# Starting addresses of the slots that TensorE reads, moved to multiples of 256 bytes

## The chip, the cores and the metric

One core of a Trainium2 chip runs the whole program. The metric is device time in microseconds (us) from the start to the end of one execution. The kernel before was run three times; the profile is one further execution of it.

## The reference

Two blocks of two layers each are applied to 512 tokens of width 1024, all in float32. What matters here is where the products are:

```python
# first block, layer l (x: [512, 1024])
h = rms_norm(x, norm_mix[l]);  z = h @ w_in[l]          # 1024 x 2560
# grouped attention, a gated recurrence in both directions and a gated convolution on parts of z
x = x + concatenate([o_att, o_hg, o_cv]) @ w_out[l]     # 1024 x 1024
h = rms_norm(x, norm_mlp[l])
x = x + square(relu(h @ w_mlp_in[l])) @ w_mlp_out[l]    # 1024 x 4096, 4096 x 1024
# second block, layer l: four mixers (sparse attention, stick breaking, gated linear, forgetting attention),
# each through a branch product 512 x 1024 times a gate; w_out_2, then the same kind of feed forward
```

## The kernel before, in words

The residual stream is kept transposed: features on the 128 partitions, 512 tokens along the free dimension, in 8 tiles. TensorE multiplies in the type float32r, which takes the leading bits of a float32 word, so each operand is split in a leading and a trailing part (`split`, L304: a copy on ScalarE and a subtraction on VectorE), and each product is made of three: leading by leading, leading by trailing, trailing by leading (`mm3`, L338).

Weights come by DMA in pieces of [128, 512] words (`wload`, L314) to slots `wr`, and are split to `wh` and `wl`. One unit holds four weight tiles of 128 x 128. `product` (L344) then takes 12 products of 512 columns with each unit: the weight tile is loaded into the array (the profile's PEld), and a part of the source is streamed past it. The source is the normed input (`xh`, `xl`: `tlater`, L366), the hidden layer of the feed forward (`hid`: `mlp`, L492), or the mixed heads (`mxh`, `mxl`: `out_proj`, L519, and the branches, L1984). `nlater` (L370) takes narrow products the other way round: a tile of `xh` or `xl` is loaded, and 256 columns of weights are streamed past it.

The feed forward of a layer runs alone: four times, 8 tiles of 128 hidden features are made from the input (8 x 8 x 3 = 192 products), and then 8 tiles of the output from these (192 products). The mixers run with projections in between, which are queued and emitted in small steps by a pacing rule (`Core.step`, L258). The order on each engine is fixed when the program is built.

Where a slot stands in SBUF follows from the pools. `Core.__init__` (L163) opens the pool `core` with the identity, the residual tiles, `xh`, `xl` and small vectors, and `corew` with the weights. `Core.scope` (L189) opens for each block a pool of small things and one of slots of [128, 512] words by purpose (`SLOTS_1`, L112, and `SLOTS_2`, L113), from which `Core.t` (L212) takes tiles; slots of the purpose k are 32 words wider. Each pool starts where the one before it ends, and a tile's size is rounded up to 32 bytes. So one small vector moves everything that stands behind it.

Of the kernel before, what the change touches and what calls it, by code (L numbers as in the profile page):

```python
# [29 lines left out]
T = 512          # tokens  # L30
D = 1024         # model width
# [5 lines left out]
AHEAD = 1        # units of weights that are loaded ahead  # L37
PARTS = 2        # steps in which the products with a unit of weights are emitted

# ---------------------------------------------------------------- constants of the shapes  # L40


def _const_parts():
    p = np.arange(128)[:, None]
    f = np.arange(128)[None, :]
    tok = np.arange(T).reshape(NT, 128).T          # [128, NT]
    parts = {}
    parts["ident"] = (p == f)
    parts["causal"] = np.where(f > p, NEG, 0.0)                       # query p, key f
    parts["far"] = np.where(f <= p, NEG, 0.0)                         # key tile two before the query's  # L50
# [3 lines left out]
    parts["sbm"] = (p < f)                                            # key p, query f  # L54
    parts["sbb"] = np.where(p >= f, NEG, 0.0)
    parts["tri"] = np.where(p >= f, -1.0, 0.0)                        # key' p, key f
# [9 lines left out]
    # axial rope of the first block: cos and signed sin for each token and feature  # L66
# [38 lines left out]
# ---------------------------------------------------------------- the program  # L105

# PSUM banks by purpose; each block has one more
BANKS = dict(pm=2, ps=2, pt=2, po=1)
# buffers of weights: as loaded, leading parts, trailing parts
WEIGHTS = dict(wr=4, wh=4, wl=3)  # L110
# slots of [128, T] words by purpose, of the first and of the second block
# [4 lines left out]
class Later:  # L116
    """work for the tensor engine that is emitted in small steps between those of something else. units: pairs of
    functions, of which the first loads weights, and the second (a generator) takes the products with them;
    finish: what to do at the end"""
# [7 lines left out]
    def load(self, n=1):  # L127
        """the weights of the next n units; how many are left to others"""
        while n and len(self.ws) < len(self.units):
            self.ws.append(self.units[len(self.ws)][0]())  # L130
            n -= 1
        return n

    def advance(self, alone=False):
        """the next step; alone: no weights are loaded for what follows"""
# [26 lines left out]
class Core:  # L162
    def __init__(self, ctx, tc, const):  # L163
# [10 lines left out]
        self.ident = self.cload("ident", self.cp)  # L174
        self.x = [self.xtile() for k in range(KT)]
# [10 lines left out]
        self.keep = tc.dram_tile([KT, 128, T], F32, name="keep")  # L186

    # -- memory
    def scope(self, ctx, name, bank, **bufs):  # L189
        """the memory of one block: slots of [128, T] by purpose, one more bank for a purpose"""  # L190
        pool = lambda n, **k: ctx.enter_context(self.tc.tile_pool(name=name + n, bufs=1, **k))
        self.ps = {bank: pool("p", space=PSUM)}
        self.bp, self.gp = pool("c"), pool("g")
        self.sp = self.bp
        self.bufs, self.turn = bufs, {}

    def next(self, name, n, times=1):
        """0, 1, .. n - 1 by turns, each some times in a row"""
# [13 lines left out]
    def t(self, tag, name="t", dt=F32, shape=None):  # L212
        """a slot of [128, T] words (k: 32 more)"""
        w = T + 32 if tag == "k" else T
# [19 lines left out]
    def vec(self, v, name, kt):  # L234
        """a vector of kt*128 features, features on the partitions"""
# [10 lines left out]
    # -- work in between  # L246
# [21 lines left out]
    def ahead(self, work, u):  # L268
        """load the weights for the unit after u of some work"""
# [13 lines left out]
    def rsqrt(self, out, ms, n):  # L283
        """1/sqrt of a small positive tile: through the logarithm, then a step of Newton's"""
# [9 lines left out]
    def norm_rows(self, weights, squares, r):  # L294
        """r = 1/sqrt of the squares' sums by weights over the partitions, plus EPS, in every row"""
# [7 lines left out]
    # -- products in float32r parts  # L303
    def split(self, hi, lo, src, hi_in=None):  # L304
        """src = hi + lo exactly, hi with the leading 12 bits"""
# [8 lines left out]
    def wload(self, pieces, a, b):  # L314
        """pieces: [(DRAM AP, their rows, their columns)]; the weights' a tiles [128, b], each in two parts"""
# [17 lines left out]
    def wcols(self, w, k0=0, kt=KT):  # L333
        """rows k0*128.. of w, [.., its columns]"""
# [9 lines left out]
    def product(self, w, n, src, finish, extra=None):  # L344
        """finish(w.T @ src) for 128 columns of n * 128 rows of weights; src: k -> the parts of its rows [128, tokens];
        extra: what else to load"""
# [19 lines left out]
    def tlater(self, w, finish=lambda p: p):  # L366
        """(x g) @ w for 128 columns, transposed: [columns, tokens]"""
        return self.product(w, KT, lambda k: (self.xh[k], self.xl[k]), finish)

    def nlater(self, w, finish=lambda ps: ps):  # L370
        """(x g) @ w for 256 columns, [tokens, columns]: two banks of two token tiles each.
        w: AP [1024, 256]; finish: of the [128, 256] products of the token tiles"""
# [27 lines left out]
    # -- residual stream, kept transposed  # L400
    def load_x(self, x, g, tag):
        """x [tokens, features] to features on the partitions; the tokens' squares are summed on the way"""
# [31 lines left out]
    def parts_of(self, k, g, x):  # L434
        """x times the norm's weight, in two parts; the row scale follows the products"""
# [9 lines left out]
    def prep(self, k, g, spill=False):  # L445
        """x[k] is final"""
# [5 lines left out]
    def rows(self, col, n=128):  # L452
        """a column [128 tokens, NT] as rows: out[p, t] = col[t], in PSUM"""
# [5 lines left out]
    # the row scale of the norm, along the tokens in every row and as columns; taken from the squares at its first use  # L459
# [1643 lines left out]
```

## Time and profile before

| | us |
|---|---|
| the three runs | 3782.01, 3783.26, 3784.59; median 3783.26 |
| the profiled execution: span from the first to the last instruction | 3781.8 |
| TensorE busy in it | 3664.3 (97%) |
| VectorE, ScalarE, GpSimd busy | 2319.6 (61%), 1900.7 (50%), 948.4 (25%) |

The median of the runs is 1.5 us above the profiled span. A row of the profile names an engine (PE is TensorE's product, PEld its weight load, DVE VectorE, ACT ScalarE, POOL GpSimd), the line of the kernel, the operation, and its tiles as output<-inputs. Of a product's two inputs, a row gives the streamed one first in the groups `pm<-xh,wh` and `pm<-hid,wh`, and in `pm<-wh,xh` of the narrow products too. The shape behind the names, 128x512, is what is streamed. Products overlap: the next one starts while the one before is still on its way, so a product's time in a row is longer than the distance between two starts.

### The profile page before, as it was taken

Reading aid. Unit: us, or ns where it says so; the run is one execution under the profiler, and the core shown is the slowest. Engines: PE = TensorE matmul, PEld = TensorE weight load, DVE = VectorE, ACT = ScalarE, POOL = GpSimd, SP = SyncE. Lnnn points to the kernel's source line nnn. Section 1 sums busy time; section 2 is a strip of 40 time slices with the busy share of each in tenths; the row PEclk is TensorE's granted clock in tenths of the full one; section 3 lists DMA queues with packets and bytes.
Section 4 is the critical chain, followed back from the end, with each engine's and each line's share of the span. In section 5 each row is a group of like instructions: output and inputs, shape, how many; then the busy total and the mean of one; then the engine's idle time right before and its main releaser. Section 6 shows DMA issues by size and latency. Waiting matters only on the chain.

```text
span 3781.8 us, 53178 instructions
## 1 busy us (share of the span) xinstructions
PE 3664.3 (97%) x18793; PEld 3006.3 (79%) x18793; DVE 2319.6 (61%) x4554; ACT 1900.7 (50%) x3940; POOL 948.4 (25%) x925
## 2 busy tenths in 40 slices
PE   8889999988999999999999999999999999999999
PEld 7757888885688887888788888887888888888887
DVE  7885333599543346787778763335588777874334
ACT  6575333466643333677654643334567844553333
POOL 4732222466122230001213122222001121222222
PEclk9999999998999999999999999999999999999999
DMA  4102333321133344212222233334312222233332
GB/s 127 53 12 79 92 95 95 114 57 31 43 93 94 93 114 129 54 46 73 67 71 68 71 112 96 96 95 123 100 34 68 71 67 71 64 104 94 96 95 87
DMA packets 561851, 306.65 MB, mean 81 GB/s; under 512 B 49978, under 2 KB 551344, under 8 KB 561584
## 3 DMA queue, kind: packets, MB, share of 16 engines
q1 hardware_dynamic: 558128, 296.95, 28.6%
q10 hardware_dynamic: 3456, 6.29, 0.5%
q8 instruction: 148, 2.42, 0.3%
q14 instruction: 119, 0.97, 0.1%
HBM read 292.68 MB, written 10.49 MB: 80 GB/s over the span
## 4 chain that ended last, share of the span: by engine, by line
PE 83%; DVE 11%; ACT 2%; DMA 1%; issue 1%; SPq 0%; POOL 0%; POOLq 0%; DVEq 0%; ACTq 0%
PE pm L340 21%; PE pm L341 21%; PE pm L342 21%; PE po L637 2%; PE pm L387 2%; PE pm L386 2%; PE pm L388 2%; DVE cy L1199 2%; PE pt L619 1%; PE pa L1014 1%; DVE X L1106 1%; DVE X L1107 1%; DVE acc L1128 1%; PE pt L1951 1%; DVE nm L584 1%
## 5 line engine op out<-in xcount | busy, mean ns | idle before, releaser
L308 DVE TENSOR_TENSOR wl<-wr,wh 128x512 fp32r<-128x512 f32 x956 | 679.8, 711 | 784.9 <-issue 377.3
L307 ACT ACTIVATE wh<-wr 128x512 fp32r<-128x512 f32 x956 | 600.3, 629 | 1084.1 <-PE pm L341 949.3
L340 PE MATMUL pm<-xh,wh 128*128 128x512 f32 x2160 | 863.7, 400 | 7.9 <-DVE zq L1040 3.9
L342 PE MATMUL pm<-xh,wl 128*128 128x512 f32 x2160 | 860.7, 399 | 8.2 <-POOL wl L327 8.2
L341 PE MATMUL pm<-xl,wh 128*128 128x512 f32 x2160 | 858.9, 398 | 0.0
L342 PEld LDWEIGHTS pm<-xh,wl 128*128 128x128 f32 x2160 | 407.2, 189 | 105.2 <-POOL wl L327 11.6
L340 PEld LDWEIGHTS pm<-xh,wh 128*128 128x128 f32 x2160 | 407.4, 189 | 102.2 <-DVE zq L1040 4.4
L341 PEld LDWEIGHTS pm<-xl,wh 128*128 128x128 f32 x2160 | 407.4, 189 | 93.5 <-issue 2.8
L341 PE MATMUL pm<-hid,wh 128*128 128x512 f32 x1024 | 402.0, 393 | 0.0
L342 PE MATMUL pm<-hid,wl 128*128 128x512 f32 x1024 | 401.2, 392 | 0.0
L340 PE MATMUL pm<-hid,wh 128*128 128x512 f32 x1024 | 400.3, 393 | 0.0
L515 POOL TENSOR_TENSOR x<-x,os 128x512 f32<-128x512 f32 x124 | 207.2, 1671 | 431.0 <-DVE os L513 430.2
L504 POOL TENSOR_TENSOR s<-r 128x512 f32<-128x512 f32 x128 | 134.0, 1047 | 593.5 <-ACT r L503 551.8
L386 PE MATMUL pm<-wh,xh 128*128 128x256 f32 x896 | 257.2, 290 | 4.7 <-ACT wh L307 3.3
L387 PE MATMUL pm<-wl,xh 128*128 128x256 f32 x896 | 257.6, 289 | 2.5 <-DVE wl L308 2.2
L388 PE MATMUL pm<-wh,xl 128*128 128x256 f32 x896 | 255.7, 287 | 0.0
L342 PEld LDWEIGHTS pm<-hid,wl 128*128 128x128 f32 x1024 | 192.4, 188 | 43.8
L340 PEld LDWEIGHTS pm<-hid,wh 128*128 128x128 f32 x1024 | 192.3, 188 | 43.5
L341 PEld LDWEIGHTS pm<-hid,wh 128*128 128x128 f32 x1024 | 192.3, 188 | 43.0
L340 PE MATMUL pm<-mxh,wh 128*128 128x512 f32 x512 | 203.2, 400 | 7.7 <-ACT mxh L307 4.9
L513 DVE TENSOR_TENSOR os<-pm,R 128x512 f32<-128x512 f32 x128 | 88.5, 692 | 196.7 <-PE pm L342 196.7
L341 PE MATMUL pm<-mxl,wh 128*128 128x512 f32 x512 | 203.6, 398 | 0.6 <-DVE mxl L308 0.6
(619 smaller groups left out, 6743.8 us busy)
## 6 DMA issues: line engine op xcount, KB each, us to landing
wr<-in_w_in_dram SPq DMA_DIRECT2D x376, 256.0 KB
wr<-in_w_ff_dram SPq DMA_DIRECT2D x256, 256.0 KB
wr<-in_w_mlp_in_dram SPq DMA_DIRECT2D x128, 256.0 KB
wr<-in_w_mlp_out_dram SPq DMA_DIRECT2D x128, 256.0 KB
wr<-in_w_out_dram SPq DMA_DIRECT2D x64, 256.0 KB
wr<-in_w_branch_dram SPq DMA_DIRECT2D x64, 256.0 KB
xo<-keep SPq DMA_DIRECT2D x32, 256.0 KB
keep<-x ACTq DMA_DIRECT2D x24, 256.0 KB
```

The source lines that it names most:

```text
L307: nc.scalar.activation(hi, src, AF.Copy)
L308: nc.vector.tensor_tensor(lo, src, (hi if hi_in is None else hi_in).bitcast(F32), op=ALU.subtract)
L340: nc.tensor.matmul(out, wh, xh, start=start, stop=False)
L341: nc.tensor.matmul(out, wh, xl, start=False, stop=False)
L342: nc.tensor.matmul(out, wl, xh, start=False, stop=stop)
L386: nc.tensor.matmul(o, self.xh[kk][:, c], h, start=f, stop=False, skip_group_check=True)
L387: nc.tensor.matmul(o, self.xh[kk][:, c], l, start=False, stop=False, skip_group_check=True)
L388: nc.tensor.matmul(o, self.xl[kk][:, c], h, start=False, stop=e, skip_group_check=True)
L504: nc.gpsimd.tensor_tensor(s, r, r, op=ALU.mult)
L513: nc.vector.tensor_tensor(s, po, R2, op=ALU.mult)
L515: (nc.vector if last and m == KT - 1 else nc.gpsimd).tensor_tensor(self.x[m], self.x[m], s, op=ALU.add)
L637: nc.tensor.matmul(*x, start=start and n == 0, stop=stop and n == len(mm) - 1, skip_group_check=True)
```

## The change

Four paddings and two wider slots. A padding of 128 bytes stands behind the identity in the pool `core`, one of 96 bytes is the first tile of the weights' pool `corew`, and one of 160 bytes in the first block's pool of small things (0, so none, in the second's). The k slots grow from 544 to 576 words, and the convolution's padded input from 542 to 576 words, of which 542 are used as before. On every engine the instructions are the same as before, in the same order; only addresses differ. (The diff also takes comments out, which is left out here; lines from L175 on stand 1 to 10 further down.)

```diff
@@ Core.__init__
         self.ident = self.cload("ident", self.cp)
+        self.pad(self.cp, 128)
         self.x = [self.xtile() for k in range(KT)]
...
         self.keep = tc.dram_tile([KT, 128, T], F32, name="keep")
+        self.pad(self.core_w, 96)
+
+    def pad(self, pool, n):
+        pool.tile([128, n // 4], F32, name="pad", tag=f"pad{n}", bufs=1)
@@ Core.scope
-    def scope(self, ctx, name, bank, **bufs):
+    def scope(self, ctx, name, bank, before, **bufs):
...
+        if before:
+            self.pad(self.bp, before)
@@ Core.t
-        w = T + 32 if tag == "k" else T
+        w = T + 64 if tag == "k" else T
@@ First.memory, Second.memory
-        K.scope(ctx, "first", "pa", **SLOTS_1)
+        K.scope(ctx, "first", "pa", 160, **SLOTS_1)
-        K.scope(ctx, "second", "ps", **SLOTS_2)
+        K.scope(ctx, "second", "ps", 0, **SLOTS_2)
@@ First.conv
-            u = K.gp.tile([128, T + 30], F32, name="u", tag="cu", bufs=1)
+            u = K.gp.tile([128, T + 64], F32, name="u", tag="cu", bufs=1)[:, :T + 30]
```

What this does to the places in the built program. Each number is the byte within a partition at which a tile starts, modulo 256; steps within a slot from one tile to the next are 512 or 1024 bytes and change nothing in it.

| what TensorE reads | before | after |
|---|---|---|
| weights `wh`, `wl` | 32 | 0 |
| normed input `xh`, `xl` | 128 | 0 |
| hidden layer, first block | 128; trailing parts of tiles 0 to 3 at 0 | 0 |
| hidden layer, second block | 32 | 0 |
| mixed heads `mxh`, `mxl`, first block | 128 | 0 |
| mixed heads, second block | 32 | 0 |
| values and weights of the attentions and of gated linear attention, second block | 32 (a few 160 and 224) | 0 (a few 192) |
| identity | 128 | 128 |
| triangle of ones (`tri`), stick breaking | 64 | 32 |

By number of float32r products of 512 columns: before, 2784 have streamed operand and weights at the same place modulo 256 (32 and 32), 8144 have 128 and 32, and 256 have 0 and 32. After it, 11,344 have 0 and 0. Of the narrow ones of 256 columns, 2688 have 32 and 128 before, 680 have 32 and 32; after it 3472 have 0 and 0.

## Rows read from the trace of the kernel before

**Rows 1.** Page: TensorE's busy time, and its granted clock in 40 slices.
```profile
PE 3664.3 (97%) x18793; PEld 3006.3 (79%) x18793; DVE 2319.6 (61%) x4554; ACT 1900.7 (50%) x3940; POOL 948.4 (25%) x925
PEclk9999999998999999999999999999999999999999
```
**Rows 2.** Busy by stage, one layer of each block (stretch, length, PE PEld DVE ACT POOL, clock, DMA, GB/s).
```profile
0.00:330.00 330.00, 284.12 (x1580) 224.04 (x1581) 260.29 (x459) 212.84 (x438) 156.40 (x172) 0.97 0.22 63
330.00:717.20 387.20, 387.20 (x1666) 311.54 (x1665) 154.45 (x233) 138.27 (x235) 102.71 (x75) 1.00 0.35 101
...
1416.00:2234.30 818.30, 803.31 (x4597) 677.02 (x4596) 621.24 (x1456) 481.09 (x1100) 122.34 (x156) 0.99 0.29 76
2234.30:2589.50 355.20, 355.20 (x1551) 289.62 (x1551) 136.29 (x208) 123.89 (x211) 94.46 (x74) 1.00 0.36 102
```
**Rows 3.** Page: the chain of work that ended last, by engine.
```profile
PE 83%; DVE 11%; ACT 2%; DMA 1%; issue 1%; SPq 0%; POOL 0%; POOLq 0%; DVEq 0%; ACTq 0%
```
**Rows 4.** Page: groups of TensorE (xcount | busy us, mean ns | idle before).
```profile
L340 PE MATMUL pm<-xh,wh 128*128 128x512 f32 x2160 | 863.7, 400 | 7.9 <-DVE zq L1040 3.9
...
L340 PE MATMUL pm<-hid,wh 128*128 128x512 f32 x1024 | 400.3, 393 | 0.0
...
L386 PE MATMUL pm<-wh,xh 128*128 128x256 f32 x896 | 257.2, 290 | 4.7 <-ACT wh L307 3.3
...
L340 PE MATMUL pm<-mxh,wh 128*128 128x512 f32 x512 | 203.2, 400 | 7.7 <-ACT mxh L307 4.9
```
**Rows 5.** Timeline of TensorE: first products of five pieces (start us, us).
```profile
448.27 0.39 PE L340 MATMUL pm<-xh,wh 128*128 128x512 f32 x1
...
493.07 0.39 PE L340 MATMUL pm<-hid,wh 128*128 128x512 f32 x1
...
537.92 0.39 PE L340 MATMUL pm<-xh,wh 128*128 128x512 f32 x1
...
2324.52 0.40 PE L340 MATMUL pm<-xh,wh 128*128 128x512 f32 x1
...
2369.34 0.40 PE L340 MATMUL pm<-hid,wh 128*128 128x512 f32 x1
...
2412.90 0.40 PE L340 MATMUL pm<-xh,wh 128*128 128x512 f32 x1
```
**Rows 6.** Busy time in the two pieces on the hidden layer (columns as in rows 2).
```profile
493.07:537.90 44.83, 44.83 (x193) 36.10 (x192) 15.87 (x24) 11.12 (x19) 12.77 (x8) 1.00 0.32 94
...
2369.34:2412.90 43.56, 43.56 (x194) 36.03 (x192) 15.87 (x24) 11.14 (x19) 12.76 (x8) 1.00 0.33 96
```
**Rows 7.** Timeline of TensorE: eleven narrow products (L1937), then 25 of `nlater`.
```profile
1888.64 0.28 PE L1937 MATMUL po<-fl,gv 128*128 128x256 f32 x1
...
1889.95 0.40 PE L340 MATMUL pm<-mxh,wh 128*128 128x512 f32 x1
...
1894.28 0.28 PE L386 MATMUL pm<-wh,xh 128*128 128x256 f32 x1
...
1897.22 0.27 PE L1951 MATMUL pt<-X,Z 128*128 128x128 f32 x1
```
**Rows 8.** Timeline and line L1014: eight float32 products, 256 columns, not float32r.
```profile
298.11 1.89 PE L1014 MATMUL pa<-pt,va 128*64 128x256 f32 x8
L1014 PE MATMUL pa<-pt,va x7: 379/379/379, 298.1 to 299.4; 128*64 128x256 f32 x7
```
**Rows 9.** Timeline of TensorE: thirteenth and 25th product of the piece at 493.07.
```profile
495.87 0.40 PE L340 MATMUL pm<-hid,wh 128*128 128x512 f32 x1
...
498.67 0.40 PE L340 MATMUL pm<-hid,wh 128*128 128x512 f32 x1
```
**Rows 10.** Groups of weight loads: weights loaded (L340), input tiles loaded (L386).
```profile
L340 PEld LDWEIGHTS pm<-xh,wh 128*128 128x128 f32 x2160 | 407.4, 189 | 102.2 <-DVE zq L1040 4.4 <-DVE z L552 3.3 <-DVE gv L1869 2.0
...
L386 PEld LDWEIGHTS pm<-wh,xh 128*128 128x128 f32 x896 | 170.6, 192 | 9.3 <-ACT wh L307 4.4 <-issue 1.5 <-DVE z L552 1.3
```

## The prediction

> **What bounds the kernel now.** I read the page's busy shares and 40 slices first. TensorE is busy for 97% of the span, and its granted clock is 0.9 or more in 39 of the 40 slices and above 0.8 in the other [rows 1], so neither idle time nor the clock is what a change of addresses could give back. Cut at the stages, the stage windows (one layer of each block stands in the rows; the other layer of a block is like it) show feed-forward stretches in which TensorE is busy without a break, and mixed stages that leave it idle for 46 us of 330 in the first block and for 15 of 818 in the second [rows 2]. The chain of waits puts 83% of the span on TensorE and 11% on VectorE [rows 3]. The groups of instructions say what TensorE does: 6480 products (three lines of 2160) stream a 512-column part of the normed input past a piece of weights, 3072 a part of the hidden layer, 1536 a part of the mixed heads, and 2688 (three of 896) are the narrow ones, which stream 256 columns of weights past a tile of the input [rows 4]. An instruction's mean time in these groups (390 to 400 ns) is a latency, since instructions overlap. What counts is the pace from start to start.
>
> That pace is in the timeline. A feed-forward stretch alternates pieces of 192 products on the input with pieces of 192 on the hidden layer (8 tiles of output x 8 tiles of rows x 3), without idle time. From the starts at which a piece begins and the next one begins [rows 5]:
> - first block, input: (493.07 - 448.27) / 192 = 233.3 ns
> - first block, hidden layer: (537.92 - 493.07) / 192 = 233.6 ns
> - second block, input: (2369.34 - 2324.52) / 192 = 233.4 ns
> - second block, hidden layer: (2412.90 - 2369.34) / 192 = 226.9 ns
>
> Same shape, same lines, same count of weight loads, same granted clock of 1.00, and DVE, ACT, POOL and DMA as busy beside the two hidden-layer pieces as makes no difference (15.87 and 15.87, 11.12 and 11.14, 12.77 and 12.76 us; share 0.32 and 0.33) [rows 6]. Yet one runs 6.7 ns a product faster. What differs is in the table of places: weights stand at 32 past a multiple of 256 bytes throughout, the input at 128 past, the first block's hidden layer at 128 (4 of its 16 slots at 0), the second block's at 32. **The fast piece is the one whose moving operand has the same place within 256 bytes as the weights that are loaded beside it.** That is the reading on which I forecast: two streams that read SBUF at once cost each other time when they are out of step.
>
> **The change, part by part.** No instruction, DMA or wait is added, removed or moved, so there is one kind of term: products times a change of pace. After the change weights, input, hidden layer and mixed heads all stand at 0. I take for all of them the pace of the one equal pair that the trace shows, 226.9 ns.
> 1. Input in the four feed-forward stretches: 4 x 768 = 3072 products x (233.4 - 226.9 = 6.5 ns) = 20.0 us. Nothing covers it; TensorE never idles there [rows 2].
> 2. Hidden layer of the first block: 1536 x (233.6 - 226.9 = 6.7) = 10.3 us, in the same stretches.
> 3. Input in the mixed stages, 6480 - 3072 = 3408, and the first block's mixed heads, 2 x 192 = 384 (at 128 too): 3792 x 6.5 = 24.7 us. Where VectorE ends the wait this buys nothing. The chain leaves TensorE 17% of 3782 = 643 us, all of it outside the feed-forward stretches (two layers of each block, 2 x (387 + 355) = 1484 us), so 28% of the other 2298 us. That makes 17.8 us the lower end and 24.7 the upper. I take 21, since 2832 of the 3408 are in the second block, whose mixed stages idle for 2% only [rows 2].
> 4. Second block's hidden layer (1536) and mixed heads (1152): an equal pair before and after, 0.
> 5. Narrow products: streamed weights go from 32 to 0 and loaded input from 128 to 0. Their pace is (1897.22 - 1894.28) / 25 = 117.6 ns; eleven products of the same width whose two operands both stand at 32 take (1889.95 - 1888.64) / 11 = 119 ns [rows 7]. Equal places buy nothing at this width. I take 0, and keep as the other end half of 226.9, 113.5 ns: 2688 x 4.1 = 11 us.
> 6. Weight loads by themselves: 189 ns where weights at 32 are loaded, 192 where input tiles at 128 are [rows 10]. A place moves a load by 3 ns at most, and the load lies beside a stream of 118 to 233 ns and more: 0. VectorE, ScalarE, GpSimd: the same instructions on slots that move by some bytes. DVE took 15.87 us for 24 instructions beside either hidden piece, whose slots it reads and writes at other places [rows 6], so 0. The DMA engines are busy for a third of such a stretch, and a piece that is 3% shorter asks them for 3% more, so that no weights come late: 0. The wider k slots and the conv slot change no count of elements: 0.
>
> Sum: 20.0 + 10.3 + 21 = 51.3 us. The profiled span is 3781.8 us, and the median of the runs stands 1.5 us above it, so I predict 3783.3 - 51.3 = **3732 us**. Bounds of the sum: 20.0 + 10.3 + 17.8 = 48 at the least, 20.0 + 10.3 + 24.7 + 11 = 66 at the most: 3735 to 3717. No row shows a pair at 0 and 0. If TensorE cares only for the difference of the two places, 0 and 0 equals 32 and 32. If multiples of 256 are also better by themselves, it is faster. For that I allow a fifth of the way from 226.9 to the 216 ns of [rows 8], 2 ns on some 11,000 wide products, 22 us below 3717, and let the range begin at 3695.
>
> A rule speaks against all of this. The Trainium skill (TensorE: Matmul & The Clock Gate, section "Step-by-step: what each phase is for") has two independent read ports on TensorE, one for the streamed operand and one for the weight load, so that loading the next weights takes nothing from the running product. The skill's SBUF — State Buffer (section "Specifications (TRN2)") gives SBUF lines of 16 bytes, and every slot stands at a multiple of 32 already. By these rules the sum is 0. The 6.7 ns between the two hidden-layer pieces do not agree with them.
>
> **Rivals.**
> - *Nothing happens* (chance 0.13). Something other than places makes the second block's hidden layer fast, for example which slots the other engines write at the time, or the change gains what it loses. For it: only one pair of places is fast in this trace, and correlation with one block is thin. Against it: input and hidden layer alternate in the same stretch of the second block, 233.4 beside 226.9 ns, and the engines beside both hidden pieces are equally busy. Time 3783 us. (This is also where the skill's two rules end.)
> - *The place 32 itself was the fast one* (0.13, slower). The streamed operand alone decides, and 0 is as slow as 128. In the first block's hidden layer the trailing parts of tiles 0 to 3 are at 0 already: of the first 12 products of each output tile 4 stream from 0, of the next 12 none does, and both dozens take 2.80 us (493.07 to 495.87 to 498.67) [rows 9]. At the fast pace the first would be 0.03 shorter. Then the input gains nothing, and the second block's 1536 hidden and 1152 mixed-head products fall from 226.9 to 233.6: 2688 x 6.7 = +18 us, 3801 us. It decides from the point at which a product at 0 takes longer than about 231.9 ns: there the gain of 6480 + 384 + 1536 = 8400 products at 233.4 equals the loss of 2688 at 226.9. Against it: the weights beside those four stood at 32, so that the pair was unequal there too, and nothing else in the trace parts the two readings.
> - *Multiples of 256 are much better* (0.08). Eight fp32 products of 256 columns take 1.89 us from first start to last end, less the last one's 379 ns, over seven: 216 ns [rows 8], and if such a product streams its columns twice, that is 512 columns in 216 ns. If the wide products came to that pace, (233.4 - 216) x 6864 + (233.6 - 216) x 1536 + (226.9 - 216) x 2688 = 119 + 27 + 29 = 175 us: 3608. Against it: neither 0, 32 nor 128 comes near it for the streamed operand.
> - *The change doesn't do what it says* is no rival with a time of its own: the places are in the table. A few constants (identity at 128, the triangle at 32) stay off; their products are too few to count.
>
> **How the numbers follow.** The forecast has 0.66, the others 0.13, 0.13 and 0.08. A measurement of this kernel tells about 0.2% (7.6 us) from no change. Faster by more: 0.66 + 0.08 = 0.74; same: 0.13; slower: 0.13. The range from 3695 to 3786 holds the forecast with its bounds and the case of no change, 0.79; the two far cases are left out.
>
> **What would show it.** Right: in the feed-forward stretches of the changed kernel all pieces of 192, on input and on hidden layer, in both blocks, last 43.6 us, each of those stretches ends 6.5 ns x 768 = 5 us earlier after its start (10 in the first block), and the mean time of the input's products in the groups drops from 400 to about 390. Narrow products stay near 118 ns. Wrong: the second block's hidden pieces lengthen to 44.8 us, or the input's stay at 44.8, or the mixed stages give back, through VectorE on the chain, what TensorE gains there.

## The result, and the profile after

The changed kernel takes **3740.51 us** (median of 4 runs, 3733.91 to 3741.22); the kernel before, run beside it, 3783.93 (4 runs, 3782.01 to 3786.28). The ratio is 0.9883, with a 95% interval from 0.9869 to 0.9897. The profiled execution took 3740.83 us with a span of 3738.3, which is 43.5 less than the span before. Forecast were 51.3 us less, 3732 in a range from 3695 to 3786. So the direction and the mechanism held, and the size was too large by 8 us. Most lines stand 8 further down than before (L340 is now L348, L386 is L394, L1937 is L1945).

The page after the change, TensorE's busy time and its granted clock in 40 slices, to be laid beside [rows 1]:

```profile
PE 3620.1 (97%) x18793; PEld 3010.6 (81%) x18793; DVE 2316.7 (62%) x4554; ACT 1900.7 (51%) x3940; POOL 947.6 (25%) x925
...
PEclk9999999999999999999999999999999999999999
```

TensorE is busy 44 us less, for as many instructions. The busy times of the other engines move by 3 us or less, as the prediction had it when it costed their moved slots at nothing. The chain that ended last is the same too, 84% on TensorE and 11% on VectorE as in [rows 3], so VectorE has not become the bound. The mean granted clock of the execution is 0.990 before and 0.989 after, so the gain is not the clock's:

```profile
PE 84%; DVE 11%; ACT 2%; issue 1%; DMA 1%; POOL 1%; SPq 0%; POOLq 0%; DVEq 0%; ACTq 0%
```

Timeline of TensorE after the change: the products with which the five pieces of [rows 5] begin and end (start us, us).

```profile
442.92 0.39 PE L348 MATMUL pm<-xh,wh 128*128 128x512 f32 x1
...
486.44 0.39 PE L348 MATMUL pm<-hid,wh 128*128 128x512 f32 x1
...
529.96 0.39 PE L348 MATMUL pm<-xh,wh 128*128 128x512 f32 x1
...
2292.56 0.39 PE L348 MATMUL pm<-xh,wh 128*128 128x512 f32 x1
...
2336.08 0.39 PE L348 MATMUL pm<-hid,wh 128*128 128x512 f32 x1
...
2379.60 0.39 PE L348 MATMUL pm<-xh,wh 128*128 128x512 f32 x1
```

The four pieces last 43.52 us each: 226.67 ns a product on the input and on the hidden layer, in both blocks. Before, three of the four lasted 44.8 and one 43.56 [rows 5]. The windows of the two hidden-layer pieces (length, then PE, PEld, DVE, ACT, POOL, granted clock, DMA share, GB/s), beside [rows 6], show that the first block's piece now equals the second's:

```profile
486.44:529.96 43.52, 43.52 (x194) 36.04 (x192) 15.87 (x24) 11.15 (x19) 12.71 (x8) 1.00 0.34 97
2336.08:2379.60 43.52, 43.52 (x194) 36.04 (x192) 15.88 (x24) 11.15 (x19) 12.68 (x8) 1.00 0.34 98
```

The stages of [rows 2], cut at the same instructions:

```profile
0.00:327.80 327.80, 284.94 (x1580) 226.17 (x1581) 260.21 (x459) 212.92 (x438) 156.19 (x172) 0.96 0.22 63
327.80:704.00 376.20, 376.20 (x1666) 311.36 (x1665) 153.47 (x233) 138.20 (x234) 102.56 (x75) 1.00 0.36 104
1391.90:2203.60 811.70, 797.29 (x4596) 677.19 (x4596) 619.99 (x1456) 481.10 (x1100) 122.83 (x156) 1.00 0.29 77
2203.60:2553.50 349.90, 349.90 (x1551) 289.54 (x1551) 136.22 (x208) 123.92 (x211) 94.17 (x74) 1.00 0.36 104
```

The feed-forward stretches became 11.0 and 5.3 us shorter (387.2 to 376.2, 355.2 to 349.9), which is what the first window's 1666 products give at 6.6 to 6.7 ns each, where both sources gain, and 768 at 6.6 (5.1 us) where the input alone does. The mixed stages, which hold most of the input's products, became only 2.2 and 6.6 us shorter. **That is where the forecast's missing 8 us are.** The groups of instructions, beside [rows 4], say the same in another way:

```profile
L348 PE MATMUL pm<-xh,wh 128*128 128x512 f32 x2160 | 855.0, 396 | 6.8 <-DVE zq L1048 2.8
...
L348 PE MATMUL pm<-hid,wh 128*128 128x512 f32 x1024 | 396.5, 389 | 0.0
...
L394 PE MATMUL pm<-wh,xh 128*128 128x256 f32 x896 | 257.8, 291 | 5.5 <-ACT wh L315 3.9
...
L348 PE MATMUL pm<-mxh,wh 128*128 128x512 f32 x512 | 202.3, 398 | 8.3 <-ACT mxh L315 5.3
```

The input's mean fell from 400 to 396 ns, not to 390: the hidden layer, which is streamed in long pieces only, came to 389, and the input, half of which is streamed in mixed stages, stopped between. And the narrow products went from 290 to 291. Their pace, from the same two products as in [rows 7]:

```profile
1866.39 0.28 PE L394 MATMUL pm<-wh,xh 128*128 128x256 f32 x1
...
1869.38 0.39 PE L1959 MATMUL pt<-X,Z 128*128 128x128 f32 x2
```

(1869.38 - 1866.39) / 25 = 119.6 ns, where 117.6 stood before. Over all narrow products that follow one another directly (distances under 150 ns, which leaves out waits and those at the lower clock) the mean went from 118.1 to 119.6 ns.

Since both executions hold the same 18,793 products in the same order, the difference can be taken apart exactly: for each product, the time to the next one's start, before less after. Summed by kind (a time over 300 ns in either execution counts as a wait):

| | forecast, us | measured, us |
|---|---|---|
| input in feed-forward stretches | 20.0 | 20.2 |
| hidden layer, first block | 10.3 | 10.6 |
| input and first block's mixed heads in the mixed stages | 21 (17.8 to 24.7) | 16.4, less 4.0 in waits after input products |
| second block's hidden layer and mixed heads | 0 | 0.6 |
| narrow products | 0 (to 11) | -1.1 |
| products of other types and widths | 0 | -3.7 |
| all other products and waits | 0 | 4.3 |
| sum | 51.3 | 43.4 |

The last three rows are partly the execution's own scatter: a second execution of the same kernel (in the experiment on the narrow products) has -2.4, -2.0 and +5.1 there and -5.6 in waits after input products, while the first two rows are the same to 0.1 us. Much of that scatter is the granted clock. Short stretches of the mixed stages run at the lower level (1.2 GHz), where a narrow product takes 210 ns, and in each execution they fall on other products: on 57 of the narrow products that follow one another before the change, on 30 after it, on 46 in the second execution. Counting only the products that ran at clock 1.00 before and after, the narrow ones lost 3.5 us in either execution, and those of other types and widths gained 0.1. So the row of -1.1 hides a loss three times as large.

### The profile page after: what moved, and what is told of

Read it like the earlier page. It is cut to its first block, busy times and chain, and to the rows that moved or that the text cites. A ratio compares the mean times of both kernels' runs of the same rounds, so it can differ in the third digit from the quotient of the medians.

```text
span 3738.3 us, 53178 instructions
## 1 busy us (share of the span) xinstructions
PE 3620.1 (97%) x18793; PEld 3010.6 (81%) x18793; DVE 2316.7 (62%) x4554; ACT 1900.7 (51%) x3940; POOL 947.6 (25%) x925
## 4 chain that ended last, share of the span: by engine, by line
PE 84%; DVE 11%; ACT 2%; issue 1%; DMA 1%; POOL 1%; SPq 0%; POOLq 0%; DVEq 0%; ACTq 0%
PE pm L348 21%; PE pm L350 21%; PE pm L349 21%; PE po L645 2%; PE pm L395 2%; PE pm L394 2%; PE pm L396 2%; DVE cy L1207 1%; PE pt L627 1%; PE pa L1022 1%; DVE X L1114 1%; DVE X L1115 1%; DVE acc L1136 1%; DVE nm L592 1%; PE pt L1959 1%
## 5 line engine op out<-in xcount | busy, mean ns | idle before, releaser
L348 PE MATMUL pm<-xh,wh 128*128 128x512 f32 x2160 | 855.0, 396 | 6.8 <-DVE zq L1048 2.8
L350 PE MATMUL pm<-xh,wl 128*128 128x512 f32 x2160 | 850.4, 394 | 7.8 <-POOL wl L335 7.8
L349 PE MATMUL pm<-xl,wh 128*128 128x512 f32 x2160 | 846.9, 393 | 0.0
L348 PEld LDWEIGHTS pm<-xh,wh 128*128 128x128 f32 x2160 | 407.5, 189 | 89.4 <-DVE z L560 3.5
L348 PE MATMUL pm<-hid,wh 128*128 128x512 f32 x1024 | 396.5, 389 | 0.0
L394 PE MATMUL pm<-wh,xh 128*128 128x256 f32 x896 | 257.8, 291 | 5.5 <-ACT wh L315 3.9
L348 PEld LDWEIGHTS pm<-hid,wh 128*128 128x128 f32 x1024 | 192.2, 188 | 39.7
L348 PE MATMUL pm<-mxh,wh 128*128 128x512 f32 x512 | 202.3, 398 | 8.3 <-ACT mxh L315 5.3
```

What stands on the lines that cost most here:

```text
L348: nc.tensor.matmul(out, wh, xh, start=start, stop=False)
L349: nc.tensor.matmul(out, wh, xl, start=False, stop=False)
L350: nc.tensor.matmul(out, wl, xh, start=False, stop=stop)
L394: nc.tensor.matmul(o, self.xh[kk][:, c], h, start=f, stop=False, skip_group_check=True)
```

## The experiments

The kernel before, run on the same occasions, took 3785.45 us (9 runs) beside the kernels of the first two questions but the last scan, 3786.24 (7) beside that scan, the moved trailing weights and the first run of the narrow products, 3783.7 (7) beside the moved trailing input and the repeated runs, and 3782.74 (7) beside the moved identity. In what follows "place" is the byte modulo 256, and "difference" the place of the streamed operand less that of the loaded one, modulo 256. A piece's pace is the time from its first product's start to the next piece's, over 192.

### Is it the difference, or the multiple of 256?

Everything at 32, by one padding:

```diff
-        self.pad(self.cp, 128)
+        self.pad(self.cp, 160)
```

> All that TensorE streams or loads as weights (input, weights, hidden layers, mixed heads) stands at 32 past a multiple of 256 bytes instead of at 0; nothing else differs from the changed kernel. Theory D (only the difference of the two places counts): every feed-forward piece of 192 products lasts 43.5 to 43.6 us (226.7 ns a product), total within 3 us of the changed kernel's 3740. Rival A (multiples of 256 are good by themselves): pieces of 44.5 us or more, total 3770 to 3800. [...]

Measured: 3740.7 us (4 runs, 3739.03 to 3744.79), ratio to before 0.9885 [0.987, 0.9899]. Timeline of TensorE in this kernel, an input piece and a hidden piece:

```profile
443.76 0.39 PE L348 MATMUL pm<-xh,wh 128*128 128x512 f32 x1
...
487.28 0.39 PE L348 MATMUL pm<-hid,wh 128*128 128x512 f32 x1
...
530.80 0.39 PE L348 MATMUL pm<-xh,wh 128*128 128x512 f32 x1
```

Both last 43.52 us, to the hundredth what 0 and 0 give. So a multiple of 256 bytes has no merit of its own: 32 and 32 is as good as 0 and 0. That ends the rivals in which an absolute place is the fast one.

The counter-test moves the weights alone back to 32 and leaves all that is streamed at 0:

```diff
-        self.pad(self.core_w, 96)
+        self.pad(self.core_w, 128)
...
-        K.scope(ctx, "first", "pa", 160, **SLOTS_1)
+        K.scope(ctx, "first", "pa", 128, **SLOTS_1)
...
-        K.scope(ctx, "second", "ps", 0, **SLOTS_2)
+        K.scope(ctx, "second", "ps", 224, **SLOTS_2)
```

> The changed kernel with the weights alone moved back to 32; input, hidden layers and all else stay at 0. Theory D: every wide pair is 0 against 32, all pieces at 231 to 234 ns as the kernel before had for its input; total 3795 to 3802, slower than the kernel before by the 18 us that its 2688 fast products then lose, since nothing gains. Rival A in the form that the streamed operand must be at a multiple of 256: pieces stay at 226.7 and the total at 3740.

Measured: 3797.1 us (6 runs, 3795.14 to 3799.14), ratio to before 1.0034 [1.0021, 1.0046]. Timeline of TensorE, the same two pieces:

```profile
448.42 0.40 PE L348 MATMUL pm<-xh,wh 128*128 128x512 f32 x1
...
493.22 0.40 PE L348 MATMUL pm<-hid,wh 128*128 128x512 f32 x1
...
538.02 0.40 PE L348 MATMUL pm<-xh,wh 128*128 128x512 f32 x1
```

44.80 us each, 233.3 ns a product, in both blocks. With every streamed operand at a multiple of 256 the kernel is slower than before, because the second block's hidden layer and mixed heads have lost their equal pair. So the streamed side's place is worth nothing by itself either.

### Which differences are slow?

Three kernels put input, first block's hidden layer and second block's hidden layer at three differences each. First 128, 64 and 32:

```diff
-        self.pad(self.cp, 128)
...
-        self.pad(self.core_w, 96)
+        self.pad(self.core_w, 224)
...
-        K.scope(ctx, "first", "pa", 160, **SLOTS_1)
+        K.scope(ctx, "first", "pa", 224, **SLOTS_1)
...
-        K.scope(ctx, "second", "ps", 0, **SLOTS_2)
+        K.scope(ctx, "second", "ps", 32, **SLOTS_2)
```

> Weights at 0; input at 128, the first block's hidden layer and its other slots at 64, the second block's at 32. Three differences in one kernel. Theory D with a period of 256: all three kinds of pieces slow, 233 to 234 ns (44.8 us), and the total above the kernel before, 3785 to 3805, since no wide product has an equal pair. If the period is 128: input at 226.7; if it is 64: input and the first block's hidden layer at 226.7, only the second block's at 232 to 234. If it is 32, or the streamed place alone counts with 32 as a good one: the second block's hidden layer at 226.7.

Measured: 3784.93 us (one run). Timeline of TensorE, first block:

```profile
445.05 0.39 PE L348 MATMUL pm<-xh,wh 128*128 128x512 f32 x1
...
489.66 0.39 PE L348 MATMUL pm<-hid,wh 128*128 128x512 f32 x1
...
533.62 0.40 PE L348 MATMUL pm<-xh,wh 128*128 128x512 f32 x1
```

At a difference of 128 the piece lasts 44.61 us (232.3 ns), at 64 it lasts 43.96 (229.0 ns), and the second block's hidden layer at 32 ran at 233.3 ns.

Then 192, 96 and 160 (the four paddings 64, 160, 0 and 160 in the places above):

> Weights at 0; input at 192, the first block's hidden layer and its other slots at 96, the second block's at 160. Theory D, period 256: all three kinds of pieces slow, 231 to 235 ns, total 3785 to 3805. Period 64: input at 226.7 and the others slow. Period 96 or a cost that grows with the distance: paces that differ among the three, the nearest to 0 modulo 256 (192, that is 64 below) the fastest.

Measured: 3795.74 us (one run); 233.3, 233.3 and 234.3 ns.

Last the small differences 16, 48 and -16. Weights start at 240 (slots of 576 words, of which the tile is words 60 and up); the hidden layers stand at 32 and 224:

```diff
-        n = 512
-        return self.core_w.tile([128, n], dt, name=tag, tag=tag, bufs=WEIGHTS[tag])[:, :a * b].rearrange("p (a b) -> p a b", a=a)
+        o = 60 if tag != "wr" else 0
+        n = 512 if tag == "wr" else 576
+        return self.core_w.tile([128, n], dt, name=tag, tag=tag, bufs=WEIGHTS[tag])[:, o:o + a * b].rearrange("p (a b) -> p a b", a=a)
...
-        K.scope(ctx, "first", "pa", 160, **SLOTS_1)
+        K.scope(ctx, "first", "pa", 192, **SLOTS_1)
...
-        K.scope(ctx, "second", "ps", 0, **SLOTS_2)
+        K.scope(ctx, "second", "ps", 224, **SLOTS_2)
```

> Weights at 240, input at 0 (16 above them modulo 256), the first block's hidden layer and other slots at 32 (48 above), the second block's at 224 (16 below). Wide pairs so far: difference 0 gives 226.7 ns, 64 gives 229.0, 128 gives 232, 32, 96, 160, 192 and 224 give 233.2 to 234.3. If what counts is a step of 64 bytes, 16 and 48 fall to 233 like 32, total 3790 to 3800. If the cost grows with the distance from 0, 16 is near 228 on both sides and 48 worse. A difference under 226.7 would show that an equal place is not the best one.

Measured: 3761.53 us (one run). Timeline of TensorE, first block: an input piece, a hidden piece and the next input piece.

```profile
446.14 0.39 PE L349 MATMUL pm<-xh,wh 128*128 128x512 f32 x1
...
489.98 0.40 PE L349 MATMUL pm<-hid,wh 128*128 128x512 f32 x1
...
534.50 0.39 PE L349 MATMUL pm<-xh,wh 128*128 128x512 f32 x1
...
578.01 0.40 PE L349 MATMUL pm<-hid,wh 128*128 128x512 f32 x1
```

The two input pieces, both at 16, last 43.84 and 43.51 us. Of the twelve whole input pieces of this kernel seven run at 226.7 ns from their 13th product on, as at a difference of 0, and five at 228.3; both kinds occur in both blocks. At 48 the hidden layer ran at 231.9 (534.50 - 489.98), at -16 at 233.3. No difference was faster than 0; the full list is in the last section.

### How many products pay for one that is out of step?

Each three products take the leading weights, the leading weights again and the trailing ones, so that the trailing weights alone at another place put one load in three out of step:

```diff
-        n = 512
-        return self.core_w.tile([128, n], dt, name=tag, tag=tag, bufs=WEIGHTS[tag])[:, :a * b].rearrange("p (a b) -> p a b", a=a)
+        o, n = (40, 576) if tag == "wl" else (0, 512)
+        return self.core_w.tile([128, n], dt, name=tag, tag=tag, bufs=WEIGHTS[tag])[:, o:o + a * b].rearrange("p (a b) -> p a b", a=a)
```

> The changed kernel with only the trailing parts of the weights moved, to 160 past a multiple of 256 (the streamed operand, at 0, is then 96 above them, the difference that cost 6.6 ns before); leading parts of the weights and all sources stay at 0. Of the three products per weight tile, the first and second use the leading part, the third the trailing one, so the load of the trailing part runs beside the second product's stream. Theory N (the partner is the load of the next product's weights): only the second product (xl or hid, line 349) is slow; a feed-forward piece lasts 43.5 + 64 x 6.6 ns = 43.9 us and the mean time in the groups rises on that line only. Rival O (a product's own weights count): the third product's (line 350) instead, same length of a piece. Rival S (any slot out of step slows both neighbours): 44.3 us. Total 3755 to 3765 by N and O.

Measured: 3803.9 us (one run). All three theories missed. Timeline of TensorE, input piece and hidden piece:

```profile
446.38 0.39 PE L348 MATMUL pm<-xh,wh 128*128 128x512 f32 x1
...
491.18 0.39 PE L348 MATMUL pm<-hid,wh 128*128 128x512 f32 x1
...
535.98 0.40 PE L348 MATMUL pm<-xh,wh 128*128 128x512 f32 x1
```

44.80 us, as long as if all loads were out of step, where 43.9 or 44.3 were expected. From start to start the three products of a group took 233, 235 and 232 ns (hidden layer): each of them is slow, also the first, whose own load and the next product's are both equal to what it streams. So a product's pace does not come from its own pair alone. Two further kernels looked for how far it reaches. In the first the trailing input (streamed by the middle one of the three) stands at 96, in the second only its last tile of eight does:

```diff
+        self.pad(self.cp, 96)
         self.xl = [self.cp.tile([128, T], F32R, name=f"xl{k}") for k in range(KT)]
+        self.pad(self.cp, 160)
```

> Only the trailing part of the input, streamed by the middle one of each three wide products, stands at 96 instead of 0; weights, leading part, hidden layer and mixed heads stay at 0. Theory T (a product pays for its own difference alone): one product in three goes from 226.7 to about 233.3, an input piece of 192 lasts 43.53 + 64 x 6.6 ns = 43.95 us, the whole about 3740 + 2160 x 5.6 ns = 3752. Theory U (one stream out of step upsets the sequence, as one third of the weights did): all three slow, the piece lasts 44.8 us, the whole about 3740 + 3072 x 6 ns + 0.6 x 3408 x 6 ns = 3771. Hidden pieces stay at 43.5 under both.

Measured: 3764.29 us (one run). Timeline of TensorE, input piece, then hidden piece, which is untouched:

```profile
446.89 0.39 PE L350 MATMUL pm<-xh,wh 128*128 128x512 f32 x1
...
491.26 0.40 PE L350 MATMUL pm<-hid,wh 128*128 128x512 f32 x1
...
534.82 0.39 PE L350 MATMUL pm<-xh,wh 128*128 128x512 f32 x1
```

The input piece lasts 44.37 us, between the two expectations; from start to start the three products of a group take 233.3, 230.8 and 229.2 ns, so all three are slow, though less than with the trailing weights moved.

```diff
-        self.xl = [self.cp.tile([128, T], F32R, name=f"xl{k}") for k in range(KT)]
+        self.xl = [self.cp.tile([128, T], F32R, name=f"xl{k}") for k in range(KT - 1)]
+        self.pad(self.cp, 96)
+        self.xl.append(self.cp.tile([128, T], F32R, name="xl7"))
+        self.pad(self.cp, 160)
```

> As before it, but only the last of the eight trailing input tiles stands at 96: 8 of the 192 products of an input piece (one of each 24) are out of step. Theory T: the piece lasts 43.53 + 8 x 6.6 ns = 43.6 us. Theory U with a short memory (the three products around it): 8 x 3 x 6.6 ns more, 43.7 us. Theory U with a long memory (once out of step, the sequence stays so to the end of the piece): 44.7 us. Whole time 3741, 3743 and 3770.

Measured: 3751.68 us (one run). Timeline of TensorE, input piece, then hidden piece:

```profile
446.01 0.39 PE L351 MATMUL pm<-xh,wh 128*128 128x512 f32 x1
...
489.78 0.40 PE L351 MATMUL pm<-hid,wh 128*128 128x512 f32 x1
...
533.32 0.39 PE L351 MATMUL pm<-xh,wh 128*128 128x512 f32 x1
```

The piece lasts 43.77 us, 0.25 more than 43.52, for 8 products out of step: 31 ns each, which is the short memory, but twice as long as expected. Averaged over the twelve pieces, the product that streams the moved tile takes 235.8 ns to the next start, the five after it 230.0, 235.9, 228.3, 232.5 and 230.9, and from the sixth on it is 226.7 again. **One product out of step by 96 costs some 33 ns, spread over six products.** With one in three, as in the two kernels before, the stretches of six overlap, and no product is left at the fast pace. What sets the size of it (the trailing weights cost more than the trailing input did) stays open. The whole time is that of one execution and 12 us above the change, of which the input pieces of the feed-forward stretches hold 12 x 0.25 = 3, all of the input at clock 1.00 holds 5.5, and 4.7 lie in products and waits at the lower clock.

### Can the narrow products be made faster?

At equal places the narrow products lost a nanosecond, so their weights were put 64 bytes off, and only theirs:

```diff
-        n = 512
-        return self.core_w.tile([128, n], dt, name=tag, tag=tag, bufs=WEIGHTS[tag])[:, :a * b].rearrange("p (a b) -> p a b", a=a)
+        o = 16 if b == 256 and tag != "wr" else 0
+        n = 512 if tag == "wr" else 576
+        return self.core_w.tile([128, n], dt, name=tag, tag=tag, bufs=WEIGHTS[tag])[:, o:o + a * b].rearrange("p (a b) -> p a b", a=a)
```

> The changed kernel with the weights of the narrow products alone (256 columns, streamed past a loaded input tile) shifted by 64 bytes within wider slots; all wide products keep equal places. From the runs so far narrow products take 119.3 ns at equal places, and 116.8 to 117.0 where the streamed operand stands 64 or 32 above the loaded one. If this is a property of the pair: 2688 x 2.5 = 6.7 us off TensorE, of which some 5 to 6.5 show: 3734 to 3736, ratio to the kernel before about 0.987. If narrow products are bound by something else and the differences seen are chance: the changed kernel's 3740.

Measured: 3735.09 us (4 runs, 3728.97 to 3737.34), ratio to before 0.9865 [0.9849, 0.9882]. The interval overlaps that of the changed kernel, which had run on another occasion, so both were run again, side by side:

> The change unaltered, timed beside the kernel with shifted narrow weights: 3740 us, ratio to before 0.988 to 0.990.

> The change with the narrow products' weights 64 bytes further on, once more, now on the same chip and beside the same runs of before as the change itself. If the narrow products' own pace is what it gained (117.5 instead of 119.3 ns, 2688 products, 4.9 us), it stands 4 to 6 us below the change, 3734 to 3736. If the earlier difference was the chip or the day, both stand at the same time.

Measured: the change 3739.68 us (4 runs, 3737.19 to 3743.72; ratio 0.9885 [0.9868, 0.9901]), with the narrow weights moved 3735.78 (4 runs, 3734.99 to 3737.7; ratio 0.9874 [0.986, 0.9889]). That is 3.9 us, just short of the 4 to 6 expected; the two sets of runs touch, and the intervals of the ratios overlap, so by the times alone it is likely rather than shown. The trace shows the cause. Timeline of TensorE in the second kernel, the 25 narrow products of [rows 7]:

```profile
1867.21 0.28 PE L395 MATMUL pm<-wh,xh 128*128 128x256 f32 x1
...
1870.16 0.27 PE L1960 MATMUL pt<-X,Z 128*128 128x128 f32 x1
```

2.95 / 25 = 118.0 ns instead of 119.6. Over all that follow one another directly the mean is 117.7 at a difference of 64, against 119.6 at 0 in the run beside it; 2688 x 1.9 = 5.1 us. Taken apart product by product as above, the narrow products at clock 1.00 account for 4.7 us, where the two executions differ by 4.5 in all. The wide products stayed at 226.67.

### Does the identity's place slow the mixed stages?

In the mixed stages a run of wide products starts slowly. Timeline of TensorE in the changed kernel, second block: a run on the mixed heads after float32 products of another width (its first, second, tenth and eighteenth product).

```profile
1855.63 0.58 PE L348 MATMUL pm<-mxh,wh 128*128 128x512 f32 x1
1856.06 0.39 PE L349 MATMUL pm<-mxl,wh 128*128 128x512 f32 x1
...
1857.90 0.39 PE L348 MATMUL pm<-mxh,wh 128*128 128x512 f32 x1
...
1859.71 0.39 PE L350 MATMUL pm<-mxh,wl 128*128 128x512 f32 x1
```

The eight products from 1856.06 take 1.84 us, 230 ns each, the next eight 1.81, 226 ns. Over all such runs on the input in the mixed stages, by the product's number in its run: the second 232.0 ns, the third 231.5, the fourth 231.2, the fifth to tenth 228 to 230, from the eleventh on 226.9. Before the change each of these numbers was 232 to 234, at the start of a run as at its end. Does the work ahead leave this behind because its own two operands stand apart? The trace says that it need not. Eleven runs on the input follow at least six float32r products of 256 or 384 columns whose two operands stand at the same place, and they start slowly too. One of them, behind products of gated linear attention (its first, sixth and ninth product):

```profile
1915.78 0.52 PE L1976 MATMUL pt<-od,gv 128*128 128x256 f32 x3
1916.14 0.40 PE L349 MATMUL pm<-xl,wh 128*128 128x512 f32 x1
...
1917.30 0.39 PE L348 MATMUL pm<-xh,wh 128*128 128x512 f32 x1
...
1917.98 0.39 PE L348 MATMUL pm<-xh,wh 128*128 128x512 f32 x1
```

The first five take 232 ns each, the next three 227. A run that starts straight behind the hidden layer's products, 512 columns wide like its own, takes 226.7 from its first product on.

One part that the change left off was the identity, at 128; the last kernel moves its padding ahead of it, so that it stands at 0 (with the narrow weights still 64 off):

```diff
-        self.ident = self.cload("ident", self.cp)
         self.pad(self.cp, 128)
+        self.ident = self.cload("ident", self.cp)
```

> The kernel with the shifted narrow weights, and besides the identity at 0 instead of 128 (its padding ahead of it, not behind it), so that the transposes, 128 columns wide, stream at 0 what they streamed at 128, past loads at 0. In the mixed stages of the changed kernel a run of wide products starts at 231 to 233 ns and comes down to 226.9 by its eleventh. If the identity's place is what upsets the starts (theory I), the first ten products of the runs get faster, and the whole stands up to 6 us below 3735, near 3729 to 3732. If a run starts slowly after any product of another width or type, whatever its place (theory W), nothing changes there: 3733 to 3737.

Measured: 3732.67 us (4 runs, 3731.82 to 3735.58), ratio to before 0.9868 [0.9851, 0.9884]. Timeline of TensorE, the same run of products:

```profile
1850.42 0.58 PE L349 MATMUL pm<-mxh,wh 128*128 128x512 f32 x1
1850.84 0.39 PE L350 MATMUL pm<-mxl,wh 128*128 128x512 f32 x1
...
1852.69 0.39 PE L349 MATMUL pm<-mxh,wh 128*128 128x512 f32 x1
...
1854.51 0.39 PE L351 MATMUL pm<-mxh,wl 128*128 128x512 f32 x1
```

1.85 us for the first eight, 1.82 for the next: no faster. Over all runs on the input the second to fourth products take 231.7, 231.6 and 231.3 ns. So the slow start does not come from the identity's place. The median is 3.1 us below the run without it (3735.78), on another occasion, with intervals of the ratio that overlap. The traces give those 3 us to the clock: the profiled executions differ by 4.0 us, products and waits at the lower clock by 4.5, and at clock 1.00 no kind of product moved by more than 0.2. The mean granted clock was 0.990 to 0.991 in these four runs, 0.988 to 0.989 in those without it. It is the fastest kernel of all, and each of its runs lies below every run of the changed kernel but one (3733.91, of eight).

## Why the prediction was right, and its size not

**The mechanism.** The forecast said that a wide product is fast when its streamed operand and the weights loaded beside it stand at the same place within 256 bytes. The kernel with everything at 32 gives the changed kernel's time, and the one with the weights alone at 32 falls back to 233.3 ns and, at 1.0034, behind the kernel before. Both ways it is the difference that decides, and not either place by itself. The Trainium skill's two read ports (TensorE: Matmul & The Clock Gate, section "Step-by-step: what each phase is for"), by which the load takes nothing from the stream, do not agree with these runs: 226.67 against 233.33 ns for the same product, by the load's place alone.

**Terms 1 and 2**, feed-forward stretches, 20.0 + 10.3 us, measured 20.2 + 10.6. Read from pieces of the same length in the same stage, they came out to a few tenths. The 226.9 ns behind them hid a little: before the change the first 24 products of each of those fast pieces took 228.3 ns behind the input's slow ones, and the rest 226.7.

**Term 3**, the mixed stages, 21 us, is the step that failed. It took the difference of pace, 6.5 ns, from long pieces and gave it to all 3792 products, less what VectorE's waits would cover. The products without a wait, 3527 of them, gained 16.4 us, 4.7 ns each, because the wide products come there in short runs: of some 260 runs on the input of three products or more fewer than half reach ten, and the first ten of a run are between the two paces. Before the change the start of a run was as slow as its middle, so the trace of before could not show it. What slows the start is open: products of another width ahead of it are enough, also where their two operands stand at the same place. The waits took back another 4.0 us behind the input's products, 2.5 of it in the first block, against 4.6 gained there by input and mixed heads together: the cover that the prediction's lower bound allowed for is there, in the stage that idles.

**Term 5**, the narrow products, costed at 0 with 11 us of gain at the other end, became a loss: 1.5 ns each where they follow directly, 3.5 us at clock 1.00. The sums of all, -1.1 us in this execution and -2.4 in the second, are smaller because fewer of them fell to the lower clock than before the change. That this and the scatter of the other rows cancel to half a microsecond, so that the whole miss looks like term 3's alone, is luck. The row was there to see: the eleven products at 32 and 32 in [rows 7] took 119 ns, those at 32 and 128 took 117.6. The prediction read it as "equal places buy nothing" where it said "equal places cost". The way round, 64 off, gives 117.6.

**Term 6**: the weight loads' rows, the other engines' busy time and the DMA's share moved as little as said. But the 3 ns by which it let a place move a load are not the place's: with everything at 0 the loads still take 189 and 193 ns. That constants left off their place were too few to count is not refuted: the identity at 0 left the starts of the runs where they were.

**The rivals.** "Nothing happens" fell with the ratio's interval. "The place 32 itself was the fast one" fell with the changed kernel's pieces at 226.67 ns, and with everything at 32 giving the same. "Multiples of 256 are much better" fell too: 0 and 0 equals 32 and 32, and the 216 ns of [rows 8] were reached by no pair.

## What to carry to other kernels

Where TensorE is the bound, take from the timeline the time from start to start in a long piece of equal products, and compare pieces that differ in nothing but where their operands stand: 3% of the pace of 512-column products lay in the difference of two addresses. Cost such a gain only for the products that run in long pieces, and price short runs between other work at less. An equal place is no rule for every width: the 256-column products wanted their two operands apart.

## What was not expected of the hardware

The pace of a 512-column float32r product, by the difference of streamed and loaded place, from the pieces of 192 at granted clock 1.00 (the 2.4 GHz level):

| difference, bytes | ns a product | where |
|---|---|---|
| 0 | 226.67 | the changed kernel; everything at 32 |
| 16 | 226.7 and 228.3 | input, seven and five of twelve pieces, from the 13th product on |
| 32 | 233.3 | hidden layer |
| 48 | 231.9 | hidden layer |
| 64 | 229.0 | hidden layer |
| 96 | 233.3 and 233.4 | input before; hidden layer |
| 128 | 232.4 and 233.3 | input, two blocks |
| 160 | 234.3 | hidden layer |
| 192 | 233.3 | input |
| 224 | 233.3 | all, with the weights at 32 |
| 240 | 233.3 | hidden layer |

It is no slope: 64 is better than 48 and 32, and only 0 and 16 are near the best. At 16 and 128 one kernel has two steady paces for the same input at the same place: at 128 one in each block, at 16 from piece to piece. So the difference alone does not fix the pace; what else does is open. At 0 it is regular to the nanosecond: 24 products take 5440.0 ns. At 2.4 GHz 226.67 ns are 544 periods and 233.33 are 560, so if a column takes one period, 32 or 48 are left over for each product. Where those 32 come from, and whether anything takes them away, no run here shows.
